# Layer 0's ConvFFN computed in the two phases of layer 1's, on one Trainium2 core

## The chip, the cores and the metric

The kernel runs on one core of a Trainium2 chip. The time is device microseconds of one execution. Two runs of the kernel before gave 3339.99 and 3344.08 us, a median of 3342.03 us. A second kernel is compared by the ratio of its time to that.

## The reference, cut to what matters

Two layers act on 1024 latent tokens and 256 context tokens of width 1024, all in float32. Each layer is an attention followed by a gated ConvFFN, and a norm ends the program. Context tokens go through layer 0 only; after layer 1's attention only the latent tokens are used.

```python
def conv_ffn(t, w_up, w_conv, b_conv, w_down):     # D = 1024, D_FF = 2816
    u = t @ w_up                                   # (n, 2 * D_FF)
    ...
    for tap in range(CONV_W):                      # 3 taps over positions
        acc = acc + up[:, tap:tap + n] * w_conv[tap]
    a, g = jnp.split(acc, 2, axis=-1)
    return (jax.nn.silu(g) * a) @ w_down
...
x = x + g2 * conv_ffn(h2, ...)
if need_ctx:                                       # layer 0 alone
    xc = xc + cg2 * conv_ffn(hc2, ...)
```

## The kernel before, in words

A float32 product is made of three matmuls: each operand is a high and a low part, and high times high, high times low and low times high add up in PSUM. Weights come as tiles of 128 x 1024 from HBM into a `raw` buffer (512 KB, one DMA on SP's queue, L111). Its high part is made by POOL (L123) or by ACT (L121), its low part by a subtraction on POOL (L125); both stand in a split buffer `wsp`. `Weights` keeps a list of what comes next, up to four splits ahead of the one in use; there are three raw and five split buffers. Tokens stand in three blocks of columns: block 0 and block 1 (512 latent tokens each) and block 2 (256 context tokens).

**Layer 0's ConvFFN** (`ffn`, L488) has 22 units of 128 hidden columns. A unit takes an `a` tile and a `g` tile of the up weights, each times all three blocks: `gemm` (L379) issues per tile 8 chunks x 3 matmuls x 3 blocks (512, 512 and 256 columns) into `u`. The three taps and the gate follow on ACT and DVE (`conv` L502 to L507, `gate` L515 to L517). Between the matmuls of the `g` tile stand those of the down product of the unit before (`down_step`, L532): groups of three into `y_ps`, each added to the resident `X` by one DVE instruction (L534). Over all units this is 2112 matmuls of 512 columns and 1056 of 256 for `u`, and 1056 and 528 for `y_ps`. Each down tile passes once. Beside it stand two pieces of work for layer 1. The modulation weights (`ada`) of four sixths are multiplied on DVE (`ada_dve`, L301 and L304), one tile a unit. And `W.sums` loads the `a` and `g` tiles of a layer 1 unit, forms four sums and differences of halves on POOL (L138 to L141) and stores them to `sscr` (L143).

**Layer 1's ConvFFN** works on the 1024 latent tokens alone and in two phases. The up product is formed as seven products of halves instead of eight: halves of the weights' 1024 inputs, and sums of them (`sscr`), meet halves of the tokens and sums of them (`token_forms`: T1 to T4 and B22). For the first 8 units the two products that need no token form (`first`, `second`) run early, into `escr`, while the forms are made; then all units pass in the order `SEQUENCE`, and the gated columns go to `gscr`. The down product (`down`, L1487) runs block by block: eight PSUM banks collect over all 22 units, so the down weights pass once for each block; `end` (L1494) adds the residual, which it loads from `xspill` one chunk at a time.

The order on each engine comes from the scheduler, except on PE (and DVE in layer 1's up phase), where it is the order of the code. SP's queue issues the DMAs in one order, and an issue that waits for a buffer holds what stands behind it.

Of the kernel before, what the change touches and what calls it, by code (L numbers as in the profile page):

```python
# [11 lines left out]
F32 = mybir.dt.float32  # L12
# [35 lines left out]
NE = 8  # L48
SEQUENCE = [x for i in range(NF) for x in (i, NE + i) if x < (NE if x == i else NF)]
NG = 5  # L50
V5 = 4
# [23 lines left out]
BUFS = {"t": 2, "R": 2, "sq": 2}  # L75
# [9 lines left out]
class Weights:  # L85
# [12 lines left out]

    def fill(self):
        while self.todo and len(self.made) < self.ahead and sum(m[1] for m in self.made) < self.whole:  # L100
            for _ in self.load(1):
                pass

    def load(self, pieces):
# [3 lines left out]
        self.count += 1  # L108
        n = src.shape[1]
# [19 lines left out]
    def sums(self, a, g, dst):  # L129

        nc = self.nc
        self.count += 1
        ra, rg = (self.raw_pool.tile([P, 1024], F32, name=f"raw{self.count}{x}", tag="raw") for x in "ag")
        for t, src in ((ra, a), (rg, g)):
            nc.sync.dma_start(out=t, in_=src)
# [21 lines left out]
def _body(nc, tc, es, a, out):  # L157
# [82 lines left out]
    xspill = dram.tile([P, KC, SEQ], F32, name="xspill")  # L240
    sscr = [dram.tile([P, 2048], F32, name=f"sscr{i}") for i in range(NF)]
    escr = [[dram.tile([P, 512], F32, name=f"escr{i}_{k}") for k in range(2)] for i in range(NE)]
    gscr = [dram.tile([P, SEQ], F32, name=f"gscr{i}") for i in range(NF)]
    xscr = dram.tile([P, KC, SEQ], F32, name="xscr")
# [108 lines left out]
    def norm_mod(yp, pool, SS, l, half, b, src, H, R=None, chunks=range(KC), inplace=False):  # L353
# [5 lines left out]
        for kc in chunks:  # L359
            t = src(kc) if inplace else pool.tile([P, 512], F32, name="t", bufs=tb[0])  # L360
            bias = mod[l][:, 24 * half + kc, s:s + 1]
            stt(out=t[:, :n], in0=src(kc), scalar=scale[:, kc, s:s + 1], in1=R[:, :n], op0=ALU.mult, op1=ALU.mult)
            S.activation(out=H[0][:, kc, :], in_=t[:, :n], func=AF.Identity, bias=bias)
            stt(out=H[1][:, kc, :], in0=t[:, :n], scalar=bias, in1=f32(H[0][:, kc, :]), op0=ALU.add, op1=ALU.subtract)  # L364
# [56 lines left out]
    def v_proj(l, bp, vtile, H, half, hook=None, units=None):  # L421
        vu = units or [W.get() for _ in range(4)]
        for i, m in enumerate(tuple(range(KC, NT // P)) + tuple(range(KC)) if ORDER[0][0] == 2 and hook else range(NT // P)):
# [7 lines left out]
    def wo_proj(l, bp, pool, Th, blocks, H, SS, np_, yp):  # L431

        tail = blocks[1:]

        def end(ps, j, b):
            b0, n = BLOCKS[b]
            s = 1 if b0 >= SEQ else 0
            if l == 0:
                xr = pool.tile([P, 512], F32, name="xr", bufs=3)
                nc.sync.dma_start(out=xr[:, :n], in_=a["xT"][:, j, b0:b0 + n])  # L440
            else:
                xr = resid[b][:, j, :]
            stt(out=X[b][:, j, :], in0=ps[:, :n], scalar=mod[l][:, 16 + j, s:s + 1], in1=xr[:, :n],
                op0=ALU.mult, op1=ALU.add)
            if l == 1:
                nc.sync.dma_start(out=xspill[:, j, b0:b0 + n], in_=X[b][:, j, :])
            sumsq(np_, SS, X[b][:, j, :], j, b0, n)

# [1194 lines left out]
```

## Time and profile before

| | us |
|---|---|
| median of two runs (3339.99 and 3344.08) | 3342.03 |
| the profiled execution | 3341.49 |
| its span | 3339.7 |
| PE busy | 3196.2 (96%) |
| DVE, POOL, ACT busy | 2148.2, 1427.6, 1142.3 |

The span runs from the first instruction's start to the last one's end; 1.8 us lie around it. In order of time the stages are: norms, v and qk of layer 0 (to 300 us), its attention (to 848), its output product (to 984.7), its ConvFFN with the first v tiles of layer 1 (to 2031), qk, v and attention of layer 1 (to 2530), its output product (to 2620), its ConvFFN's up phase (to 3064) and down phase (to 3339.7).

### The profile page before, as it was taken

How to read it: one execution, taken by the hardware profiler on the slowest of the kernel's cores; microseconds unless marked ns; L12 is line 12 of the kernel's file. 1: busy time of each engine (PE TensorE's matmuls, PEld its weight loads, DVE VectorE, ACT ScalarE, POOL GpSimd, SP SyncE). 2: the span in 40 equal slices, each digit the busy share in tenths (PEclk: the TensorE clock that was granted, in tenths of full speed). 3: DMA queues.
4: the chain of work that ended last, by engine and by line, in shares of the span. 5: the costliest groups of instructions: out<-in, count | busy, mean ns of one | idle time of the engine just before them, and what ended most of it. 6: DMA issues, size and time to landing. Idle time of an engine off the chain costs nothing.

```text
span 3339.7 us, 43069 instructions
## 1 busy us (share of the span) xinstructions
PE 3196.2 (96%) x15896; PEld 2638.8 (79%) x15896; DVE 2148.2 (64%) x3537; ACT 1142.3 (34%) x1990; POOL 1427.6 (43%) x916
## 2 busy tenths in 40 slices
PE   8999889999989999999999989999999989999988
PEld 4888767777677888888888868888898778888876
DVE  6577388887666666666666684325996667666351
ACT  3121177777222111111111132115994344444011
POOL 2214166666323333333433442222665345446753
PEclk9999999999999999999999999999999999999999
DMA  7564343432422223232322236646884243434452
GB/s 262 166 211 164 126 113 106 115 114 71 142 71 95 101 89 101 90 112 72 115 79 89 89 113 226 237 167 166 194 203 147 98 145 136 149 127 158 164 179 82
DMA packets 213665, 449.47 MB, mean 135 GB/s; under 512 B 25424, under 2 KB 87248, under 8 KB 213456
## 3 DMA queue, kind: packets, MB, share of 16 engines
q1 hardware_dynamic: 212448, 446.41, 41.6%
q8 instruction: 126, 2.06, 0.3%
q14 instruction: 83, 0.68, 0.1%
q10 hardware_dynamic: 1008, 0.32, 0.0%
HBM read 331.28 MB, written 115.34 MB: 134 GB/s over the span
## 4 chain that ended last, share of the span: by engine, by line
PE 62%; DVE 5%; POOL 2%; DMA 2%; issue 1%; ACT 1%; SPq 0%; DVEq 0%; POOLq 0%; ACTq 0%
PE u L379 16%; PE w_ps L1349 11%; PE y_ps L532 9%; PE y_ps L1487 6%; PE qk_ps L379 6%; PE wo_ps L379 4%; PE o L1208 2%; PE wo_ps L464 1%; PE s L1133 1%; PE tl L1160 1%; DVE Hl L364 1%; PE v_ps L391 1%; PE v_ps L390 1%; PE v_ps L389 1%; POOL wsp L125 1%
## 5 line engine op out<-in xcount | busy, mean ns | idle before, releaser
L125 POOL TENSOR_TENSOR wsp<-raw,wsp 128x1024 fp32r<-128x1024 f32 (+2 forms) x283 | 645.3, 2287 | 253.3 <-ACT wsp L121 241.2
L123 POOL TENSOR_SCALAR wsp<-raw 128x1024 fp32r<-128x1024 f32 (+1 forms) x195 | 220.5, 1135 | 1148.0 <-PE u L379 485.5
L379 PE MATMUL u<-Hh,wsp 128*128 128x512 f32 (+1 forms) x2112 | 506.6, 359 | 0.0
L534 DVE SCALAR_TENSOR_TENSOR X<-y_ps,mod,X 128x256 f32<-128x256 f32 (+1 forms) x528 | 343.5, 660 | 247.4 <-PE y_ps L532 246.4
L379 PEld LDWEIGHTS u<-Hh,wsp 128*128 128x128 f32 x2112 | 371.8, 190 | 73.4 <-issue 0.9
L532 PE MATMUL y_ps<-Gh,wsp 128*128 128x512 f32 (+1 forms) x1040 | 365.0, 365 | 12.8 <-DVE X L534 11.9
L379 PE MATMUL qk_ps<-Hh,wsp 128*128 128x512 f32 (+1 forms) x1408 | 329.4, 365 | 0.0
L502 ACT ACTIVATE acc<-u,c_ffn_conv 128x1024 f32<-128x1024 f32 (+2 forms) x89 | 73.7, 875 | 681.2 <-PE u L379 681.0
L379 PE MATMUL u<-Hl,wsp 128*128 128x512 f32 (+1 forms) x1056 | 278.1, 359 | 0.0
L379 PEld LDWEIGHTS qk_ps<-Hh,wsp 128*128 128x128 f32 x1408 | 239.9, 188 | 43.8
L1349 PE MATMUL w_ps<-FT,wsp 128*128 128x512 f32 x1056 | 252.4, 393 | 4.8 <-DVE t L1415 4.8
L532 PEld LDWEIGHTS y_ps<-Gh,wsp 128*128 128x128 f32 x1040 | 198.8, 191 | 56.3 <-DVE X L534 16.3
L1487 PE MATMUL y_ps<-g,wsp 128*128 128x512 f32 x1056 | 242.8, 392 | 0.0
L1349 PEld LDWEIGHTS w_ps<-FT,wsp 128*128 128x128 f32 x1056 | 199.2, 189 | 49.4 <-DVE t L1415 5.2
L1487 PEld LDWEIGHTS y_ps<-g,wsp 128*128 128x128 f32 x1056 | 199.8, 189 | 42.1 <-issue 0.6
L304 DVE SCALAR_TENSOR_TENSOR ada<-raw,c_cvec,ada 128x512 f32<-128x512 f32 x224 | 178.3, 830 | 58.7 <-DMA raw<-in_ada_w_dram 57.6
L379 PEld LDWEIGHTS u<-Hl,wsp 128*128 128x128 f32 x1056 | 179.4, 190 | 25.7
L812 ACT ACTIVATE E<-E,st 128x1280 f32<-128x1280 f32 x128 | 175.3, 1369 | 68.1 <-DVE st L807 67.2
L532 PE MATMUL y_ps<-Gl,wsp 128*128 128x256 f32 (+1 forms) x520 | 188.7, 363 | 2.2 <-DVE Gl L517 2.2
L822 POOL TENSOR_TENSOR E<-E,E 128x1280 f32<-128x1280 f32 x64 | 188.4, 2943 | 5.3
L379 PE MATMUL qk_ps<-Hl,wsp 128*128 128x512 f32 (+1 forms) x704 | 183.6, 364 | 0.0
L807 DVE CUSTOM_DVE_ANT_0 E<-sl,zero,st 128x1024 f32<-128x1024 f32 x128 | 163.7, 1280 | 20.2 <-PE sl L805 19.7
(317 smaller groups left out, 6215.7 us busy)
## 6 DMA issues: line engine op xcount, KB each, us to landing
raw<-in_ada_w_dram SPq DMA_DIRECT2D x96, 512.0 KB
raw<-in_up_dram SPq DMA_DIRECT2D x66, 512.0 KB
raw<-in_down_dram SPq DMA_DIRECT2D x66, 512.0 KB
raw<-sscr SPq DMA_DIRECT2D x44, 512.0 KB
raw<-in_wqk_dram SPq DMA_DIRECT2D x32, 512.0 KB
q<-qscr SPq DMA_DIRECT2D x256, 64.0 KB
q<-qscr SPq DMA_DIRECT2D x64, 256.0 KB
vscr<-vt SPq DMA_DIRECT2D x56, 256.0 KB
```

What stands on the lines that cost most here:

```text
L123: nc.gpsimd.tensor_scalar(out=sp[:, 0, c:c + n], in0=raw[:, c:c + n], scalar1=1.0, scalar2=1.0, op0=ALU.mult, op1=ALU.mult)
L125: nc.gpsimd.tensor_tensor(out=sp[:, 1, c:c + n], in0=raw[:, c:c + n], in1=f32(sp[:, 0, c:c + n]), op=ALU.subtract)
L304: stt(out=accs[v], in0=tv[:, kk, :], scalar=scol[:, kc, v:v + 1], in1=accs[v], op0=ALU.mult, op1=ALU.add)
L379: T.matmul(out=ps, lhsT=w[:, kc, :], rhs=H[b][s][:, kc, :], start=(kc == 0 and i == 0), stop=(kc == KC - 1 and i == 2))
L502: S.activation(out=acc[:, x0:x1], in_=u[:, x0 - t0:x1 - t0], func=AF.Identity, scale=w[:, 1:2], bias=w[:, 3:4])
L532: T.matmul(out=y[:, :n], lhsT=w[:, j, :], rhs=g[:, b0 - g0:b0 - g0 + n], start=(i == 0), stop=(i == len(seq) - 1))
L534: stt(out=x, in0=y[:, :n], scalar=mod[l][:, 40 + j, s:s + 1], in1=x, op0=ALU.mult, op1=ALU.add)
L807: V.tensor_tensor_reduce(out=E[j][:, :SEQ], in0=ps, in1=zero.broadcast_to([P, SEQ]), op0=ALU.add, op1=ALU.min, scale=-1.0, scalar=m, accum ...
L812: S.activation(out=E[j], in_=E[j], func=AF.Exp, scale=-1.0, bias=m, accum_out=sm)
L822: G.tensor_tensor(out=E[0], in0=E[0], in1=E[1], op=ALU.add)
L1349: T.matmul(out=ps, lhsT=w, rhs=form(kc, s), start=(start and kc + i == 0), stop=(kc == 3 and i == 2), skip_group_check=not start)
L1487: T.matmul(out=ys[j], lhsT=w[:, j, :], rhs=g[:, k % 4, s, :], start=(k == 0 and i == 0), stop=(k == NF - 1 and i == 2))
```

## The change

One function `ffn` now serves both layers, with these parts for layer 0.

**Phase A**, 22 units: the pair of tiles is loaded (`add_pair`), high parts on ACT, low parts on POOL (`high_low`, L150 and L151). 48 matmuls of 256 columns make the context's columns. For the first 11 units the early products follow (24 of 512 columns), and the pair's four sums go from the raw tiles to `sscr` (`sums`, L185 to L190).

**Phase B**: the seven-product up of the latent tokens in the order 11, 0, 12, 1, ... A unit below 11 has 60 matmuls of 512 columns; one from 11 on has 84, and its sums are made on POOL as its tiles pass (`add_forms`), with no store.

**Phase C**: the down product by blocks, in the order 2, 0, 1, so that the down weights pass three times. The `ada` tiles are multiplied in blocks 2 and 0 (`ADA_AT`), the sums for 8 units of layer 1 are made in block 1 (`SUM_AT`). Block 1 begins with `turn` (the `ada` columns), a norm and `write0` (layer 1's first operand).

`u` and `y_ps` of layer 0 become `w_ps`: 1848 matmuls of 512 columns and 1056 of 256 for the up product (before 2112 and 1056); the down product keeps 1056 and 528.

In layer 1 the sums of the units from 8 on are now made as their tiles pass. In both layers the residual of block 0 and block 1 is loaded into `X` at the start of the block, and gated tiles use two rotating buffers (six before). The output products load `X` for both blocks at their start. After layer 0's ConvFFN high parts are made on ACT.

```diff
-NE = 8
-NG = 5
-V5 = 4
+NE = (11, 8)
+RAW = 3
+SEQUENCE = [[x for i in range(NF) for x in (ne + i, i) if x < (ne if x == i else NF)] for ne in NE]
+NG = 4
+ADA_AT = [(0, 6), (0, 12)] + [(1, k) for k in range(3, 17)]
+SUM_AT = [(2, k) for k in range(2, 18, 2)]
+V5 = 1
...
+    def halves(self, kind, i, a, g, dst, raw):
+        tt = self.nc.gpsimd.tensor_tensor
+        if i == 0:
+            raw.extend(self.pair(a, g))
+        ra, rg = raw[:2]
...
+        if kind == "pair":
+            self.high_low(raw[i], 1024)
+            if i and dst is not None:
+                self.sums(ra, rg, dst)
+            return
+        if i == 0:
+            raw.append(self.sum_pool.tile([P, 1024], F32, name=f"sum{self.count}", tag="sum"))
+            s = raw[2]
+            tt(out=s[:, 512:], in0=g1, in1=g2, op=ALU.add)
+            tt(out=s[:, :512], in0=s[:, 512:], in1=a1, op=ALU.subtract)
+        elif i == 1:
+            tt(out=a1, in0=a1, in1=g1, op=ALU.subtract)
+            tt(out=a2, in0=a2, in1=raw[2][:, :512], op=ALU.subtract)
+        self.high_low((raw[2], ra, g2)[i] if i < 2 else g2, (1024, 1024, 512)[i])
...
-            x = X[b0 // 512][:, j, :]
-            stt(out=x, in0=y[:, :n], scalar=mod[l][:, 40 + j, s:s + 1], in1=x, op0=ALU.mult, op1=ALU.add)
...
-                gemm(units[1], H, outs[1], extra if ops else None)
...
-                for k in range(i, NF if i == NF - 2 else i + 1):
-                    W.sums(a["up"][1, k], a["up"][1, NF + k], sscr[k])
...
+            for i in range(NF if l == 0 else ne):
+                aa = W.get()
+                if l == 0:
+                    gg, ps = W.get(), bank(1)
+                    for k, u in enumerate((aa, gg)):
+                        gemm(u, H, [(2, ps[:, CTX * k:CTX * k + CTX])])
...
+                if i < ne:
+                    x, p1 = first(aa)
+                    late.append((i, aa, x, p1))
...
+                def end(j):
+                    if b < 2:
+                        x = out_[b][:, j, :]
+                    else:
+                        x = small()[:, :n]
+                        nc.sync.dma_start(out=x, in_=xspill[l][:, j, b0:b0 + n])
+                    stt(out=x, in0=ys[j][:, :n], scalar=mod[l][:, 40 + j, b // 2:b // 2 + 1], in1=x, op0=ALU.mult, op1=ALU.add)
+                    if l == 0:
+                        nc.sync.dma_start(out=xscr[:, j, b0:b0 + n], in_=x)
...
+                for k in range(2, NF - 3):
+                    sp = W.get()
+                    load_g(1)
+                    for j in range(KC):
+                        down(k, j, sp)
+                    if hook:
+                        hook(at, k)
...
+        for i in range(NF if l == 0 else NE[1]):
+            if l == 0:
+                W.add_pair(a["up"][0, i], a["up"][0, NF + i], sscr[0][i] if i < NE[0] else None)
...
+        for i in SEQUENCE[l]:
+            if i < NE[l]:
+                for src in (sscr[l][i][:, :1024], sscr[l][i][:, 1024:], a["up"][l, NF + i][:, 512:]):
+                    W.add(src)
+            else:
+                W.add(a["up"][l, i])
+                W.add_forms(a["up"][l, i], a["up"][l, NF + i])
+        for at in range(3 - l):
+            for k in range(NF):
+                W.add(a["down"][l, k])
+                if l == 0 and (at, k) in ADA_AT:
+                    add_quarters(q1, 1)
```

Three places show how instructions move. On POOL, in the middle of layer 0's ConvFFN, a unit of before has three high parts (L123), three low parts (L125) and the four sums of a layer 1 unit that has tiles of its own:

```order
257 L123 TENSOR_SCALAR wsp_10915<-raw_10913 128x1024
258 L125 TENSOR_TENSOR wsp_10915<-raw_10913,wsp_10915 128x1024
259 L138 TENSOR_TENSOR raw113g<-raw113g 128x512
260 L139 TENSOR_TENSOR raw113g<-raw113a,raw113g 128x512
261 L140 TENSOR_TENSOR raw113a<-raw113g,raw113a 128x512
262 L141 TENSOR_TENSOR raw113a<-raw113a 128x512
```

On POOL in phase A of the change, two units:

```order
253 L151 TENSOR_TENSOR wf_9903<-raw99a,wf_9903 128x1024
254 L151 TENSOR_TENSOR wf_9906<-raw99g,wf_9906 128x1024
255 L185 TENSOR_TENSOR raw99g<-raw99g 128x512
256 L186 TENSOR_TENSOR raw99g<-raw99a,raw99g 128x512
257 L187 TENSOR_TENSOR raw99a<-raw99g,raw99a 128x512
258 L188 TENSOR_TENSOR raw99a<-raw99a 128x512
259 L151 TENSOR_TENSOR wf_10017<-raw101a,wf_10017 128x1024
```

The sums now overwrite the tiles (`raw99a`, `raw99g`) whose low parts PE waits for, and the high parts are gone from POOL. SP's queue for a unit of before issues the pair of a layer 1 unit, its four stores and the unit's own four tiles:

```order
411 L135 DMA raw113a<-in_up_dram 128x1024
412 L135 DMA raw113g<-in_up_dram 128x1024
413 L143 DMA sscr_131<-raw113g 128x512 x2
414 L143 DMA sscr_131<-raw113a 128x512 x2
415 L111 DMA raw_11229<-in_up_dram 128x1024
416 L111 DMA raw_11234<-in_up_dram 128x1024
417 L111 DMA raw_11239<-in_down_dram 128x1024
```

and in phase A of the change (`sscr` are the stores of the sums, `escr` and `gscr` those of the early products and of the context's gated columns):

```order
430 L190 DMA sscr_8_179<-raw97g 128x512 x2
431 L190 DMA sscr_8_179<-raw97a 128x512 x2
432 L156 DMA raw99g<-in_up_dram 128x1024
433 L156 DMA raw101a<-in_up_dram 128x1024
434 L668 DMA escr_7_0_204<-p_9977 128x512
435 L650 DMA gscr_7_134<-t 128x256
436 L668 DMA escr_6_1_203<-t 128x512
437 L190 DMA sscr_9_180<-raw99g 128x512 x2
```

The `g` tile of the next unit is issued behind the four stores of this one. On DVE a unit of before ends with the taps (L507), the gate and the additions to the resident `X`:

```order
1520 L507 SCALAR_TENSOR_TENSOR acc<-u_9969,c_ffn_conv,acc 128x255
1521 L515 TENSOR_TENSOR acc<-acc 128x1280
1522 L517 TENSOR_TENSOR Gl<-acc,Gh 128x1280
1523 L534 SCALAR_TENSOR_TENSOR X_7909<-y_ps,mod_90,X_7909 128x256
1524 L507 SCALAR_TENSOR_TENSOR acc<-u_10287,c_ffn_conv,acc 128x1023
```

and at the passage from block 2 to block 0 of phase C in the change (L776 is the end of one PSUM bank of block 2, L1237 a step of the `ada` product, L555 the low part of a gated tile of block 0, L375 the sum of squares):

```order
1712 L1237 SCALAR_TENSOR_TENSOR rows<-raw_14544,c_cvec,rows 128x512 x2
1713 L776 SCALAR_TENSOR_TENSOR t<-w_ps,mod_90,t 128x256
1714 L1237 SCALAR_TENSOR_TENSOR rows<-raw_14544,c_cvec,rows 128x512
1715 L375 TENSOR_TENSOR SS<-SS,sq 128x256
1716 L1237 SCALAR_TENSOR_TENSOR rows<-raw_14544,c_cvec,rows 128x512
1717 L776 SCALAR_TENSOR_TENSOR t<-w_ps,mod_90,t 128x256
1718 L555 TENSOR_TENSOR g_14395<-t,g_14395 128x512 x4
1719 L375 TENSOR_TENSOR SS<-SS,sq 128x256
1720 L1237 SCALAR_TENSOR_TENSOR rows<-raw_14665,c_cvec,rows 128x512 x2
1721 L776 SCALAR_TENSOR_TENSOR t<-w_ps,mod_90,t 128x256
```

Between the ends of the eight banks stand `ada` steps and gated tiles of the next block.

## Rows read from the trace of the kernel before

**Rows 1.** Windows: length, then busy us and count of each engine, granted clock, DMA:
```profile
core 0: us, PE busy (x) PEld busy (x) DVE busy (x) ACT busy (x) POOL busy (x), PEclk, DMA share, GB/s
984.70:2031.00 1046.30, 1014.33 (x5094) 851.68 (x5093) 684.32 (x925) 176.84 (x214) 388.03 (x245) 0.98 0.28 96
...
2620.00:3064.00 444.00, 428.89 (x1842) 350.19 (x1841) 295.00 (x315) 197.61 (x257) 203.93 (x88) 0.97 0.40 138
3064.00:3339.70 275.70, 251.86 (x1093) 206.44 (x1092) 106.54 (x97) 45.96 (x73) 158.09 (x86) 0.95 0.42 145
```
**Rows 2.** Waits of PE, 984 to 2031 us: total us, times, longest us:
```profile
PE y_ps L532 <- DVE X L534: 14.0, 10, 3.7
PE rn_ps L339 <- DVE SS L327: 7.0, 1, 7.0
```
**Rows 3.** Chain of waits, two stretches of matmuls: start us, us, what and count:
```profile
1890.70 0.69 PE y_ps L532 x3
...
3079.85 91.36 PE y_ps L1487 x403
```
**Rows 4.** Timeline of PE, matmuls of 256 columns: start us, us, what, count:
```profile
985.00 0.28 PE L379 MATMUL u<-Hl,wsp 128*128 128x256 f32 x1
985.12 0.40 PE L379 MATMUL u<-Hh,wsp 128*128 128x256 f32 x2
```
**Rows 5.** Groups by line and shape: count, then busy us, mean ns, idle before:
```profile
L125 POOL TENSOR_TENSOR wsp<-raw,wsp 128x1024 fp32r<-128x1024 f32 x237 | 600.7, 2540 | 228.0 <-ACT wsp L121 217.5
...
L534 DVE SCALAR_TENSOR_TENSOR X<-y_ps,mod,X 128x512 f32<-128x512 f32 x352 | 259.6, 749 | 159.2 <-PE y_ps L532 159.0
...
L304 DVE SCALAR_TENSOR_TENSOR ada<-raw,c_cvec,ada 128x512 f32<-128x512 f32 x224 | 178.3, 830 | 58.7 <-DMA raw<-in_ada_w_dram 57.6
...
L534 DVE SCALAR_TENSOR_TENSOR X<-y_ps,mod,X 128x256 f32<-128x256 f32 x176 | 84.9, 483 | 88.2 <-PE y_ps L532 87.4
...
L121 ACT CAST wsp<-raw 128x1024 fp32r<-128x1024 f32 x66 | 69.3, 1050 | 67.0 <-PE w_ps L1349 60.2 <-issue 6.7
...
L1297 DVE TENSOR_TENSOR g<-t,g 128x512 fp32r<-128x512 f32 x39 | 55.7, 1486 | 8.5 <-ACT g L1296 8.5
```
**Rows 6.** Timeline of POOL, the sums of one unit:
```profile
1588.43 1.30 POOL L138 TENSOR_TENSOR raw153g<-raw153g 128x512 f32<-128x512 f32 x1 [13.16 <-DMA raw153g<-in_up_dram]
1589.81 1.30 POOL L139 TENSOR_TENSOR raw153g<-raw153a,raw153g 128x512 f32<-128x512 f32 x1
...
1592.56 1.30 POOL L141 TENSOR_TENSOR raw153a<-raw153a 128x512 f32<-128x512 f32 x1
```
**Rows 7.** Timeline of SP's DMA issues, the same unit:
```profile
1584.68 0.33 SPq L135 DMA_DIRECT2D raw153g<-in_up_dram  x1
...
1592.50 1.70 SPq L143 DMA_DIRECT2D sscr<-raw153a  x2
1594.30 3.06 SPq L111 DMA_DIRECT2D raw<-in_up_dram  x2
```
**Rows 8.** Windows around PE's wait of 3.7 us, columns as in the first group:
```profile
1039.50:1046.00 6.50, 3.44 (x15) 2.36 (x13) 6.50 (x6) 1.22 (x2) 4.71 (x2) 0.81 0.00 0
1046.00:1060.00 14.00, 14.00 (x61) 11.65 (x62) 9.94 (x15) 0.00 (x0) 5.18 (x4) 0.85 0.53 189
```
**Rows 9.** Waits of PE, 2620 to 3340 us:
```profile
PE rn_ps L339 <- DVE SS L327: 17.7, 3, 10.6
```
**Rows 10.** Chain of waits, the end of the 10.6 us wait:
```profile
3196.92 0.33 SPq L111
...
3197.34 3.90 DMA t<-xspill
```
**Rows 11.** Timeline of DVE, one addition of 128 x 512 at two places:
```profile
969.18 0.68 DVE L327 TENSOR_TENSOR SS<-SS,sq 128x512 f32<-128x512 f32 x1
...
981.76 2.88 DVE L327 TENSOR_TENSOR SS<-SS,sq 128x512 f32<-128x512 f32 x1
```
**Rows 12.** Timeline of POOL beside the second of them:
```profile
981.38 2.71 POOL L125 TENSOR_TENSOR wsp<-raw,wsp 128x1024 fp32r<-128x1024 f32 x1
```

More of the change, by code (lines that the diff above doesn't have):

```diff
@@ L47 @@
 NS = 7
[L48 to L51 removed]
+NE = (11, 8)
+NP1 = (2, 4)
+RAW = 3
[4 more added lines that the diff above has]
+V5 = 1
 NEB = 5
@@ L97, in add, with add_pair, add_forms @@
         self.todo.append((src, split))
+    def add_pair(self, a, g, dst=None):
+        raw = []
+        self.todo.extend((("pair", i, a, g, dst, raw), None) for i in range(2))
+    def add_forms(self, a, g):
+        raw = []
+        self.todo.extend((("forms", i, a, g, None, raw), None) for i in range(3))
     def fill(self):
@@ new lines, in ada_columns, with norm1 @@
+    def ada_columns():
+        for n in range(4):
+            ps = yp.tile([P, 512], F32, name="ada_ps", tag="y")
+            for j in range(4):
+                for v in range(2):
+                    c = 2 * (2 * j + v)
+                    T.matmul(out=ps[:, c:c + 2], lhsT=rows[0][:, 2 * n + v, j * P:j * P + P], rhs=ones[:, :2],
+                             start=True, stop=True)
+            ada_end(1, n, ps[:, :16].rearrange("p (j v c) -> p j v c", v=2, c=2)[:, :, :, 0], 2)
+    def norm1(b, R, x):
+        norm_mod(yp, np_, SS, 1, 0, b, x, H1[b], R, inplace=True)
@@ L1340, in write @@
             nc.sync.dma_start(out=out[:, kc, 512 * b:512 * b + 512], in_=x[:, kc, :])
-    def bank():
-        return bp.tile([P, 512], F32, name="w_ps", tag="b")
-    def product(ps, sp, c, form, start):
-        for kc in range(4):
-            h, l = (sp[:, s, (4 * c + kc) * P:(4 * c + kc + 1) * P] for s in range(2))
-            for i, (w, s) in enumerate(((h, 0), (h, 1), (l, 0))):
-                T.matmul(out=ps, lhsT=w, rhs=form(kc, s), start=(start and kc + i == 0), stop=(kc == 3 and i == 2),
-                         skip_group_check=not start)
@@ L1455, in _body @@
-    while rest:
-        fill()
-    manual.close()
-    gtags = ("T2", "T1", "Hh0", "Hl0", "Hh1", "Hl1")
-    loads = deque((b, k) for b in range(2) for k in range(NF))
-    gs, Rs, xo = {}, [], []
-    def load_g(n, eng=V):
-        for _ in range(n):
-            if not loads:
-                return
-            b, k = loads.popleft()
-            if k % 4 == 0:
-                gs[b, k // 4] = hp.tile([P, 4, 2, 512], F32R, name=f"g{k // 4}", tag=gtags[k // 4])
-            t = small()
-            nc.sync.dma_start(out=t, in_=gscr[k][:, 512 * b:512 * b + 512])
-            split(gs[b, k // 4], k % 4, t, eng)
```

746 lines of the change are left out of this document (341 added, 405 removed).

## Prediction

> **What bounds the kernel now.** I read the windows by stage first [rows 1]. In the stretch of layer 0's ConvFFN (984.7 to 2031 us, with the first v tiles of layer 1) PE is busy for 1014.3 of 1046.3 us, while DVE has 684 and POOL 388. So PE sets the time there, and matmuls taken away count in full unless something else comes late. What a matmul costs is its distance from the next one, not its busy time (busy spans overlap). In the chain of waits, 403 matmuls of 512 columns take 91.36 us, 0.2267 each, and in the ConvFFN of layer 0 three take 0.69, 0.23 each [rows 3]. Matmuls of 256 columns follow each other after 0.12 us, with a new weight tile each [rows 4].
>
> By these the stretch needs 3408 x 0.2267 (2112 u, 1056 y, 240 v) + 1584 x 0.12 + some 10 us of small ones = 973 us. It takes 1046.3, so 73 us are lost: 21 in the two longest kinds of wait [rows 2], some of it to the clock behind them [rows 8], the rest to slightly wider distances and the end of the stage. The question is whether the new form loses more or less than 73.
>
> **What is removed.** The up product keeps 1848 of 2112 wide matmuls: 264 x 0.2267 = 59.9 us (60.7 at 0.23). All else on PE stays: 1056 + 528 narrow ones, 1056 wide ones down, the ada columns. The stretch needs 913 us. On DVE the 352 + 176 additions to X go (260 + 85 us [rows 5]); they were mostly beside PE's work, so I cost them at nothing beyond the 14.0 us of waits that PE had for them, which are in the 73. The 22 high parts per pass go to ACT at 1.05 us, which has 177 of 1046 us filled: nothing.
>
> **What is added, and where it may be late.** I go through the phases and price the losses that replace the 73.
>
> *Phase A, units 0 to 10.* PE needs 48 x 0.12 + 24 x 0.2267 = 11.2 us a unit. One unit's tiles go through a chain, since the sums overwrite both tiles and the next g tile is issued behind the four stores: 0.44 from the last sum's end (1593.86) to the next issue, 3.75 from issue to POOL's first use (1584.68 to 1588.43), 1.05 on ACT, 2.54 of subtraction, and 5.43 for four sums (1588.43 to 1593.86) [rows 5 to 7]. That is 13.2 us, and up to a microsecond more because two loads start together. Nine units at 2 to 3 us over PE are 18 to 27 us; the two units that are ready at the start cover some 10. I take 13 (0 to 32: no wait if the chain overlaps better, and 32 in the rival below).
>
> *Phase A, units 11 to 21.* PE needs 5.76 us, POOL 2 x 2.54 = 5.1, three raw buffers (3.75 + 1.05 + 2.54) x 2 / 3 = 4.9. Nothing is left over: 5 us (0 to 19).
>
> *Phase B.* Two steps need 144 x 0.2267 = 32.6 us on PE; POOL has at most seven subtractions and four sums, 17.8 + 5.5 = 23.3 us. Covered. For the last token forms before it and the start I put 3 + 5 us (2 to 18).
>
> *Phase C, block 2.* A unit is 24 x 0.12 = 2.88 us, POOL 2.54, the buffers 7.34 / 3 = 2.45. The down weights now come three times, and this is where the pace is highest: 6 us (0 to 20; the far end is a rival).
>
> *From block 2 to block 0.* PE's next banks wait for the ends of block 2. On DVE these stand between ada steps (the order shows two to four before each), a group of four gated tiles, and sums of squares; each ada tile is issued on SP behind the store of an earlier end. From the last unit's first bank on, DVE has about 14 steps x 0.83 + 4 x 1.49 + 8 x 0.48 + 8 x 0.4 = 25 us, and at least two load times of 3.75 in series on top [rows 5 to 7]: the eighth bank comes at about 33 us. PE could use it at 8.6 + 7 x 1.36 = 18 us. Loss 14 us (0 to 25).
>
> *Block 0 behind it.* A unit is 5.44 us; DVE has 4 x 0.83 + 1.49 = 4.8, and that wait has given the loads a lead: 4 (0 to 30). *Block 1*: eight pairs for layer 1, each 13.2 us a pair against 10.9 for two units, less a lead of about 16: 5 (0 to 24). *turn, norm and the first operand*: 6. *End of the stage and start*: 6 + 4, as before.
>
> The sum is 13 + 5 + 8 + 6 + 14 + 4 + 5 + 6 + 10 = 71 us, about the 73 of before. So nearly the whole 60 us stays: 60 + 2 = 62.
>
> *Layer 1.* PE waits 10.6 us for the sum of squares in its down phase [rows 9], and the chain behind that wait ends in a residual load (issue at 3196.92, then 3.90 us of transfer) that SP issued late [rows 10]. Now the residual is there from the start of the block, and what remains (an end, a square, an addition, some 2 us) lies under the four banks that PE does first: minus 10. The sums that units 8 to 21 now make on the way add 5.5 us of POOL to steps of 84 x 0.2267 = 19 us, of which POOL holds 8.7: covered. So minus 10 (minus 14 to plus 5). The output products: 0 (minus 2 to plus 3).
>
> Against the profiled execution: 3341.5 - 62 - 10 = 3269.5 us. The median of the runs is 0.5 above it, so **3270 us**.
>
> **Where the skill and the trace meet.** After PE's wait of 3.7 us at 1039.5 us the granted clock is 0.81 and then 0.85 over 14 us [rows 8], that is, part of the time at 1.2 GHz instead of 2.4. [...] The same addition on DVE takes 0.68 us at one place and 2.88 at another, where POOL's subtraction runs from 981.38 for 2.71 us [rows 11, 12]. The Trainium skill, "SBUF — State Buffer", section "Who interferes with whom", says that a DVE instruction with two SBUF inputs and a GpSimd one that reads SBUF exclude each other for a whole instruction; the trace agrees. Both speak against this change and are rivals below.
>
> **The rivals.**
> 1. *All is hidden.* The chains run under PE as they do in layer 1's up phase, where PE is busy for 428.9 of 444 us [rows 1], and 30 us are lost: 3229 us. Against it: the 13.2 us of chain against 11.2.
> 2. *The raw buffers bound phase A and block 1.* The second of the two loads in rows 7 was issued 2.7 us after the first, when a store of the tile had landed (3.06 us for two issues of 0.33). If each cycle waits for that, it is 15.9 us: phase A 9 x 4.7 - 10 = 32 instead of 13, its second half 7.5 a unit instead of 5.76 (19 instead of 5), block 1 19 more. 52 us are given back: 3322. Against it: the order has the a tile one unit ahead, so one load alone is late.
> 3. *DVE is held by POOL in block 0.* Each unit there has one subtraction of 2.54. If an ada step meets it each time, DVE needs 4.8 + 2.5 = 7.3 us against 5.44: 14 x 1.9 = 26 instead of 4, so 3292.
> 4. *The clock.* If waits keep the granted clock at 0.85 through the second half of phase A, block 2 and block 0 (63 + 63 + 120 us), these take 1/0.85 of their time, 43 us more: 3313. Against it: where a chain is the bound, slower matmuls only fill the wait.
> 5. *Slower than before: the down weights come one at a time.* SP's queue in phase C holds gated tiles, stores and ada tiles between them. If they keep only one weight load under way in block 2, a unit takes 3.75 + 1.05 + 2.54 = 7.34 us instead of 2.88: 22 x 4.46 = 98 us more, 3368. It decides from 6.2 us a unit (72 / 22 above 2.88). Against it: three buffers, and loads that the order has ahead.
>
> That the change doesn't remove the matmuls can be left out: the code has 264 fewer.
>
> **How the numbers follow.** The forecast has 0.55, with a range of its own of 3245 to 3298 (the terms of 13 and 14 us at their ends). Rival 1 has 0.12, rival 2 0.15, rival 3 0.08, rival 4 0.06, rival 5 0.04. The range is 3222 (rival 1, with a little less lost) to 3330 (rival 2 and 4 within it); below and above lie 0.2. A 2% difference, about what a measurement of this kernel can tell from no change, lies at 3275.2 and 3408.9. The forecast is faster by that in some 0.6 of its cases (0.33), rival 1 always, rival 3 seldom: 0.46. Slower by 2% needs rival 5 and more: 0.02. The rest is 0.52.
>
> **What would show it.** Layer 0's stretch should take about 984 us, 62 less, with u and y_ps replaced by w_ps. Phase A's units should be 13 to 14 us apart from the third or fourth on, with PE waiting for POOL's low part of g. A wait of PE for DVE's L776 should stand between blocks 2 and 0, 10 to 20 us in all. In layer 1's down phase the 10.6 us wait should be gone. The forecast is wrong if units of block 2 take over 4 us, if phase A's first half takes over 170 us (123 without a wait), or if layer 1 loses time to POOL. Were phase B to show waits for POOL, the sums made on the way would be mis-priced.

## The result and the profile after

The changed kernel took 3466.39 us (two runs, 3463.97 and 3468.82) against 3342.03: 1.0372 times the time before, 95% interval 1.0328 to 1.0417. The forecast was 3270, so not even the sign was right. The profiled execution took 3468.82 us, its span is 3467.0, 127.3 us longer than before. By the first matmul of each stage:

| stage | before | after | forecast |
|---|---|---|---|
| layer 0's output product | 138.2 | 157.1 | 138 |
| layer 0's ConvFFN and layer 1's first v tiles | 1046.1 | 1112.8 | 984 |
| layer 1's up phase | 448.0 | 497.0 | 448 |
| layer 1's down phase | 272.0 | 267.6 | 262 |

Between these stages nothing moved by more than 3.2 us. The windows of after split the ConvFFN into its phases; columns as in [rows 1]. In order: the output product of layer 0, phase A's first 11 units, its last 11, phase B, phase C's blocks 2, 0 and 1, then layer 1's up and down:

```profile
843.40:1000.70 157.30, 141.80 (x654) 110.33 (x654) 90.68 (x130) 39.99 (x72) 43.48 (x24) 0.89 0.46 153
...
1000.70:1157.50 156.80, 133.47 (x804) 118.72 (x803) 92.62 (x102) 62.26 (x97) 113.39 (x63) 0.95 0.60 193
1157.50:1220.70 63.20, 63.20 (x529) 63.20 (x528) 35.54 (x47) 34.94 (x50) 52.00 (x24) 1.00 0.63 193
...
1220.70:1660.60 439.90, 390.43 (x1586) 312.17 (x1586) 286.54 (x274) 167.02 (x215) 252.81 (x121) 0.93 0.34 113
1660.60:1744.60 84.00, 68.93 (x529) 67.21 (x528) 42.64 (x43) 32.54 (x48) 57.03 (x25) 0.91 0.73 240
1744.60:1880.90 136.30, 128.10 (x529) 102.52 (x529) 88.94 (x98) 40.59 (x56) 56.64 (x23) 0.94 0.61 203
1880.90:2053.60 172.70, 146.49 (x603) 116.42 (x604) 58.56 (x61) 44.90 (x61) 96.13 (x54) 0.89 0.62 214
...
2702.30:3199.30 497.00, 445.86 (x1860) 361.11 (x1859) 332.92 (x314) 197.51 (x257) 310.08 (x148) 0.95 0.36 117
3199.30:3467.00 267.70, 248.44 (x1078) 203.05 (x1076) 107.95 (x96) 43.44 (x71) 152.53 (x82) 0.96 0.44 148
```

By the prediction's distances PE needs 123, 63, 359, 63, 120 and 120 us in the phases from A to C. Phase B is thus 81 us over its need and block 1 is 53 (some 10 of it the small matmuls that the prediction counted apart). PE is idle for 49.5 us of phase B, and the clock is 0.93 there; layer 1's up phase went from 0.97 [rows 1] to 0.95 and is 49 us longer.

The largest waits of PE in phase A (two rows), phase B (two), block 1 (one) and layer 1's up phase (two): total us, times, longest.

```profile
PE w_ps L608 <- ACT p L620: 11.6, 2, 8.2
PE w_ps L428 <- POOL wf L151: 5.7, 4, 1.9
...
PE w_ps L608 <- DVE work L708: 31.5, 9, 4.3
PE w_ps L608 <- DVE t L696: 18.0, 11, 4.3
...
PE w_ps L767 <- POOL wsp L142: 16.7, 8, 3.3
...
PE w_ps L608 <- DVE work L708: 27.2, 8, 4.3
PE w_ps L608 <- DVE t L696: 11.1, 8, 2.0
```

Phase B's waits are not for POOL, whose work was added, but for DVE: for two additions that read a PSUM bank (L696, L708) in which PE is to go on. The timelines of after show one such wait (POOL, DVE, then PE; start us, length us):

```profile
1411.90 3.39 POOL L151 TENSOR_TENSOR wf<-sum,wf 128x1024 fp32r<-128x1024 f32 x1
1415.25 2.82 POOL L151 TENSOR_TENSOR wf<-raw161a,wf 128x1024 fp32r<-128x1024 f32 x1
...
1413.54 5.08 DVE L630 SCALAR_TENSOR_TENSOR work<-uh,c_ffn_conv,work 128x512 f32<-128x512 f32 x2
1418.73 1.23 DVE L730 TENSOR_TENSOR work<-work 128x1024 f32<-128x1024 f32 x1
1419.87 0.69 DVE L708 TENSOR_TENSOR work<-w_ps,t 128x512 f32<-128x512 f32 x1
...
1430.17 1.53 DVE L630 SCALAR_TENSOR_TENSOR work<-uh,c_ffn_conv,work 128x512 f32<-128x512 f32 x2
...
1414.38 2.88 PE L608 MATMUL w_ps<-FB,wsp 128*128 128x512 f32 x12
1420.70 2.97 PE L608 MATMUL w_ps<-FT,wsp 128*128 128x512 f32 x12 [3.44 <-DVE work L708]
```

Two taps that take 1.53 us with POOL idle (1430.17) take 5.08 beside two low parts on POOL, and the low part of a sum takes 3.39 where [rows 5] has 2.54. Taps, gate and low part have both inputs in SBUF. L708 has one in PSUM and takes its usual 0.69, but stands behind them in DVE's order. PE has one product, 12 x 0.2267 = 2.72 us (here 1414.38 to 1417.2), before it needs the bank back. It comes 3.44 us late.

### The profile page after: what moved, and what is told of

Read it like the earlier page. It is cut to its first block, busy times and chain, and to the rows that moved or that the text cites. A ratio compares the mean times of both kernels' runs of the same rounds, so it can differ in the third digit from the quotient of the medians.

```text
span 3467.0 us, 43539 instructions
## 1 busy us (share of the span) xinstructions
PE 3192.5 (92%) x15632; PEld 2624.0 (76%) x15632; DVE 2130.6 (61%) x3294; ACT 1400.1 (40%) x2388; POOL 1730.6 (50%) x984
## 4 chain that ended last, share of the span: by engine, by line
PE 49%; POOL 16%; issue 13%; DVE 11%; DMA 8%; ACT 3%; SPq 0%; POOLq 0%; ACTq 0%; DVEq 0%
PE qk_ps L428 9%; PE w_ps L767 9%; POOL wsp L142 6%; PE w_ps L608 6%; POOL wf L151 4%; PE wo_ps L428 3%; PE o L1038 3%; PE sl L987 3%; PE o L1429 2%; PE v_ps L438 2%; PE v_ps L439 2%; PE v_ps L440 2%; PE tp L1014 2%; PE w_ps L428 1%; DMA raw<-in_down_dram 1%
## 5 line engine op out<-in xcount | busy, mean ns | idle before, releaser
L767 PE MATMUL w_ps<-g,wsp 128*128 128x512 f32 (+1 forms) x2640 | 575.8, 380 | 50.1 <-POOL wsp L142 23.2
L767 PEld LDWEIGHTS w_ps<-g,wsp 128*128 128x128 f32 x2640 | 474.4, 195 | 150.1 <-POOL wsp L142 28.8
L138 ACT CAST wsp<-raw 128x1024 fp32r<-128x1024 f32 (+1 forms) x213 | 195.0, 928 | 365.1 <-PE w_ps L608 158.2
L428 PE MATMUL qk_ps<-Hh,wsp 128*128 128x512 f32 x1280 | 319.7, 372 | 0.0
L608 PE MATMUL w_ps<-FT,wf 128*128 128x512 f32 x1200 | 288.1, 392 | 4.4 <-DVE t L696 4.3
L608 PEld LDWEIGHTS w_ps<-FT,wf 128*128 128x128 f32 x1200 | 226.5, 189 | 53.9 <-DVE t L696 4.8
L555 DVE TENSOR_TENSOR g<-t,g 128x512 fp32r<-128x512 f32 (+1 forms) x102 | 135.8, 1372 | 211.6 <-ACT g L554 211.6
L630 DVE SCALAR_TENSOR_TENSOR work<-work,c_ffn_conv 128x1023 f32<-128x1023 f32 x88 | 170.9, 1943 | 98.1 <-ACT work L627 97.2
L608 PE MATMUL w_ps<-Hh,wsp 128*128 128x512 f32 x528 | 177.6, 402 | 8.4 <-ACT p L620 8.4
L987 PE MATMUL sl<-kst,q 128*128 128x512 f32 x512 | 160.0, 436 | 1.6 <-DVE st L989 1.5
```

Source lines behind the costliest of these rows:

```text
L138: nc.scalar.copy(out=sp[:, 0, c:c + n], in_=raw[:, c:c + n])
L428: T.matmul(out=ps, lhsT=w[:, kc, :], rhs=H[b][s][:, kc, :], start=(kc == 0 and i == 0), stop=(kc == KC - 1 and i == 2))
L555: eng.tensor_tensor(out=form[:, kc, 1, :], in0=x, in1=f32(form[:, kc, 0, :]), op=ALU.subtract)
L608: T.matmul(out=ps, lhsT=w, rhs=form(kc, s), start=(start and kc + i == 0), stop=(kc == 3 and i == 2), skip_group_check=not start)
L630: stt(out=acc, in0=u, scalar=convw[:, l, c, k:k + 1], in1=acc, op0=ALU.mult, op1=ALU.add)
L767: T.matmul(out=ys[j][:, :n], lhsT=w[:, j, :], rhs=g[:, k % 4, s, :], start=(k == 0 and i == 0), stop=(k == NF - 1 and i == 2))
```

## The experiments

Stage times of all runs in us, as in the table above. C2, C0 and C1 are the blocks of phase C, wo the output product of layer 0, and "time" is that of the profiled execution. Each of these kernels was run once, after twice and g1 four times:

| run | wo | A | B | C2 | C0 | C1 | up 1 | time |
|---|---|---|---|---|---|---|---|---|
| after | 157.1 | 220.0 | 440.0 | 84.0 | 136.3 | 172.7 | 497.0 | 3468.8 |
| e1_no_form_sums | 157.0 | 223.1 | 363.2 | 84.3 | 133.9 | 172.5 | 436.0 | 3328.9 |
| e2_reads_first | 157.2 | 223.2 | 380.5 | 81.7 | 133.6 | 171.4 | 449.2 | 3353.9 |
| e3_halves | 151.6 | 227.4 | 410.5 | 83.5 | 136.2 | 168.9 | 480.3 | 3417.0 |
| f1_block1_no_pool | 141.4 | 223.7 | 381.4 | 82.2 | 135.9 | 167.8 | 451.0 | 3345.3 |
| f2_order_and_halves | 138.5 | 227.3 | 363.8 | 82.4 | 136.1 | 170.9 | 443.2 | 3322.9 |
| f3_sums_in_qk | 140.3 | 223.3 | 380.5 | 81.8 | 133.7 | 140.1 | 450.7 | 3330.6 |
| f4_three_p1 | 143.3 | 222.6 | 380.4 | 81.8 | 133.9 | 173.0 | 447.6 | 3341.4 |
| g1_sums_split | 137.4 | 225.9 | 364.5 | 79.8 | 135.4 | 154.8 | 442.5 | 3300.8 |
| g2_phaseA_no_pool_sums | 142.2 | 188.4 | 363.8 | 80.8 | 136.1 | 171.5 | 443.3 | 3287.0 |
| g3_sums_all_qk | 138.1 | 225.4 | 363.7 | 79.9 | 133.6 | 138.7 | 442.9 | 3302.5 |

The kernel before took 3338.31 beside the first group (e), 3342.83 beside the second (f), and 3344.45 (median of seven) beside the third (g).

**e1: the sums on the way left out.**

```diff
-            tt(out=s[:, 512:], in0=g1, in1=g2, op=ALU.add)
...
-        self.high_low((raw[2], ra, g2)[i] if i < 2 else g2, (1024, 1024, 512)[i])
+        self.high_low((rg, ra, g2)[i], (1024, 1024, 512)[i])
```

> The changed kernel, but the four sums that POOL forms as tiles pass (L173 to L177, units from 11 on in layer 0 and from 8 on in layer 1) are left out: the raw tiles stand in for them. In the changed kernel layer 0's phase B took 439.9 us and layer 1's up phase 497. Theory 1 (DVE's taps with two SBUF inputs and POOL's operations exclude each other, so DVE reads a PSUM bank late and PE waits): POOL has 5.5 us less in each such step, phase B 385 to 400 us, layer 1's up phase 455 to 465, whole 3370 to 3390. Theory 2 (the order of DVE's own instructions alone, with the drain before L708, makes the waits): both phases unchanged within 5 us. Theory 3 (weights come late through POOL and the raw buffers): the waits of PE would name POOL and fall; 10 us in each phase at most, since PE's waits there name DVE.

Phase B came down by 76.8 us and layer 1's up by 61, both by more than theory 1 had expected. The window of phase B has PE without a gap, for as many matmuls, and the group of the two taps that stand ahead of L708 is back at its length:

```profile
1223.00:1586.20 363.20, 363.20 (x1588) 296.63 (x1587) 258.42 (x272) 166.55 (x213) 183.22 (x80) 1.00 0.42 137
```
```profile
L622 DVE SCALAR_TENSOR_TENSOR work<-uh,c_ffn_conv,work 128x512 f32<-128x512 f32 x88 | 65.6, 746 | 1.5
```

The same group in after, and in before:

```profile
L630 DVE SCALAR_TENSOR_TENSOR work<-uh,c_ffn_conv,work 128x512 f32<-128x512 f32 x88 | 125.5, 1426 | 1.5
```
```profile
L1368 DVE SCALAR_TENSOR_TENSOR work<-uh,c_ffn_conv,work 128x512 f32<-128x512 f32 x44 | 35.8, 813 | 0.7
```

The 76.7 us between the two windows of phase B are 49.5 of idle PE and 27.2 of longer busy time (390.43 against 363.20), at 0.93 and 1.00 of the clock. The sums cost all that the two stages lost.

**e2: the additions that PE waits for before the taps.** This keeps every sum and changes only the order on DVE.

```diff
                 product(y, f, 0, of("T2"), True)
-                fill()
                 V.tensor_tensor(out=u2, in0=y, in1=p1, op=add)
+                fill(3)
...
                 product(y, f, 0, of("T3"), False)
-                while rest:
-                    fill()
                 V.tensor_tensor(out=ug[:, hi], in0=y, in1=q, op=add)
+                fill(0)
```

> The changed kernel with another order on DVE in the seven-product phase: the additions that read PSUM (L696, L700, L708) come before the leftover taps of the step before, instead of behind them. Same work on every engine. Theory 1: DVE's taps stay as long as they are (mean 1.4 us for 512 columns of uh), but they no longer stand before the reads; phase B 400 to 425 instead of 439.9, layer 1's up phase 465 to 485 instead of 497. Theory 2: all waits of that kind go, phase B 365 to 380, layer 1's up phase 440 to 450, and taps are as long as in the kernel before. Theory 3: no change.

Phase B fell by 59.5 us and layer 1's up by 47.8. Neither theory had it whole: the times are about those of theory 2, but the taps do not get shorter as it had them, they are longer than in after:

```profile
L630 DVE SCALAR_TENSOR_TENSOR work<-uh,c_ffn_conv,work 128x512 f32<-128x512 f32 x88 | 152.5, 1733 | 1.6
```
```profile
PE w_ps L608 <- DVE t L693: 4.3, 1, 4.3
PE w_ps L608 <- ACT p L620: 4.0, 8, 0.5
PE w_ps L608 <- DVE work L703: 2.8, 8, 0.5
```

So the length of the taps is not the price. What costs is a lengthened tap that stands ahead of a read of PSUM which PE waits for.

**e3: low parts in halves of 512 columns**, so that POOL holds DVE for less at a time; the order is that of after.

```diff
-        nc.gpsimd.tensor_tensor(out=sp[:, 1, :], in0=src, in1=f32(sp[:, 0, :]), op=ALU.subtract)
+        for c in range(0, n, 512):
+            nc.gpsimd.tensor_tensor(out=sp[:, 1, c:c + 512], in0=src[:, c:c + 512], in1=f32(sp[:, 0, c:c + 512]), op=ALU.subtract)
```

> The changed kernel with each low part on POOL made in two halves of 512 columns (all low parts after layer 0's attention): POOL's total rises by some 0.2 us a tile, its longest single instruction falls from 2.5 to 1.3 us. Theory 1: a DVE instruction waits for at most half as long a POOL instruction, so PE's waits on DVE in phase B (49.5 us) fall by a third to a half: phase B 415 to 425, layer 1's up phase 475 to 485. Theory 2: no change. Theory 3 (POOL's throughput): phase B and block 1 a little slower, 2 to 10 us.

It took 29.5 us off phase B, somewhat more than expected, and 16.7 off layer 1's up: less than half of what the order gives.

**e4: the kernel before, with its layer 1 sums made on the way** (units 8 to 21), nothing else of the change. **g4: the kernel before, with e2's order.**

```diff
             W.add(a["up"][1, i])
+            W.add_forms(a["up"][1, i], a["up"][1, NF + i])
+            continue
```

> The kernel before with one part of the change alone: in layer 1 the sums of units 8 to 21 are made on POOL as their tiles pass; layer 0 makes only the first 8 units' sums. Layer 1's up phase took 447.8 us before and 497 in the changed kernel. Theory 1: 483 to 500 us, and DVE's taps from SBUF grow as in the changed kernel; layer 0's ConvFFN (1046 us) unchanged or up to 5 us shorter; whole 3375 to 3395. Theory 2: unchanged, 3335 to 3345. Theory 3: 455 to 465, with waits of PE for POOL.

> The kernel before, with only the order on DVE changed in layer 1's up phase (reads of PSUM before leftover taps). There POOL makes no sums, and PE's waits for DVE are 4.8 us in all. If the order matters only together with POOL's sums, the up phase stays at 440 to 449 us (448.0 before) and the whole within 0.3% of before; if the order is worth something by itself, 425 to 438.

e4 took 3387.7 us, 49.4 more than the kernel before beside it. Layer 1's up went from 448.0 to 502.3 us, while layer 0's ConvFFN, rid of 14 units' sums, gained only 9.0 (1037.1). The up phase is just over the range of theory 1. The same two waits are there as in after:

```profile
PE w_ps L1395 <- DVE work L1473: 24.9, 7, 4.3
PE w_ps L1395 <- DVE t L1461: 17.2, 8, 7.8
```

g4 took 3339.43 us, layer 1's up 444.8. That is 3.2 us less than before, no more than the 3.4 by which four runs with the same up phase differ (e2, f1, f3 and f4: 447.6 to 451.0). The order decides where POOL makes sums beside the taps; without them no gain of it is shown.

**f1 to f4** all have e2's order, and the first tiles of the output product's weights issued ahead of its other loads (`W.fill()` before `Th`). In after these stood on SP behind the loads of the attention's result; the timeline of SP's issues, of after and then of before:

```profile
842.29 13.29 SPq L1214 DMA_DIRECT2D ots<-oscr  x14
855.67 0.39 SPq L489 DMA_DIRECT2D X<-in_xT_dram  x1
...
868.81 0.39 SPq L128 DMA_DIRECT2D raw<-in_wo_dram  x1
```
```profile
845.53 0.37 SPq L111 DMA_DIRECT2D raw<-in_wo_dram  x1
```

In all runs with that line (f and g) the output product takes 137.4 to 143.3 us instead of 157.

**f1: block 1 without POOL's sums**, loads and stores kept.

```diff
-            W.sums(*W.pair(a["up"][1, i], a["up"][1, NF + i]), sscr[1][i])
+            ra, rg = W.pair(a["up"][1, i], a["up"][1, NF + i])
+            for k, t in enumerate((ra[:, :512], rg[:, 512:], rg[:, :512], ra[:, 512:])):
+                nc.sync.dma_start(out=sscr[1][i][:, 512 * k:512 * k + 512], in_=t)
```

> Reads first on DVE as in the run of that name (whole 3352 us span, output product of layer 0 157.2 us, block 1 of phase C 171.4 us of which PE's matmuls need some 128), and two more edits in other stages. (1) The first four weight tiles of layer 0's output product are issued ahead of the loads of the attention's outputs. If SP's queue order made that stage longer (138.2 before, 157.2 in the changed kernel), it takes 138 to 146; if the four 1 MB loads of X or ACT are at fault, 152 to 158. (2) In block 1 the eight pairs are loaded and stored, but the four sums on POOL are left out. If POOL's time bounds block 1 (two low parts and four sums, some 10.6 us of 10.9 for two units), it takes 130 to 140; if the three raw buffers and the wait for the stores bound it, 155 to 172. Whole: 3290 to 3315 by POOL and queue, 3335 to 3350 by the rivals.

Block 1 took 167.8 us, against 171.4 in e2. POOL's sums are not its bound. The issues of f1 on SP show its pace:

```profile
1904.13 0.33 SPq L128 DMA_DIRECT2D raw<-in_down_dram  x1
1905.04 0.38 SPq L156 DMA_DIRECT2D raw278a<-in_up_dram  x1
...
1911.24 0.33 SPq L128 DMA_DIRECT2D raw<-in_down_dram  x1
...
1919.23 0.33 SPq L128 DMA_DIRECT2D raw<-in_down_dram  x1
1920.13 0.38 SPq L156 DMA_DIRECT2D raw280a<-in_up_dram  x1
```

Two down tiles are issued every 15.1 us (1904.13 to 1919.23), where PE needs 10.9 for two units. A pair holds two of the three raw buffers until its four stores are through. POOL's timeline of f1 has the low parts of the down tiles:

```profile
1901.74 2.37 POOL L142 TENSOR_TENSOR wsp<-raw,wsp 128x1024 fp32r<-128x1024 f32 x1 [5.92 <-ACT wsp L138]
1908.81 2.40 POOL L142 TENSOR_TENSOR wsp<-raw,wsp 128x1024 fp32r<-128x1024 f32 x1 [4.70 <-ACT wsp L138]
1916.85 2.35 POOL L142 TENSOR_TENSOR wsp<-raw,wsp 128x1024 fp32r<-128x1024 f32 x1 [5.64 <-ACT wsp L138]
```

Each of the three issues of a down tile above comes 0.02 or 0.03 us after the end of such a low part (1904.11, 1911.21 and 1919.20), that of the tile before. So the down tiles pass one at a time: load, high part and low part of one take 7.1 to 8.0 us here, and two of them make the 15.1. That the pair's two buffers are what keeps the next load back fits this, and f3 below has no pairs there, but no run had a fourth buffer.

**f3: the eight units' sums moved to layer 1's qk product.**

```diff
-SUM_AT = [(2, k) for k in range(2, 18, 2)]
+SUM_AT = []
...
+            W.sums(*W.pair(a["up"][1, g], a["up"][1, NF + g]), sscr[1][g])
```

> Reads first on DVE, the output product's weights issued first, and the eight pairs of layer 1's sums moved from block 1 of phase C to the qk stage of layer 1, one for each of its eight steps (POOL is lightly used there). Block 1 135 to 142 instead of 171.4. The qk stage takes 261 us up to the attention; if its raw buffers and DMA have room for 16 MB more it stays within 3 us, if not it grows by 10 to 30 (three raw buffers, 21.6 us of holding times in 25.7). Whole 3295 to 3320.

Block 1 fell to 140.1 us, 31 less, but the stretch from the qk product to the attention went from 261.3 to 282.5: two thirds of the gain are paid back.

**f4: a third buffer for the saved early product** (`NP1 = (3, 4)`), against the 8.2 us wait of PE for the copy L620 in phase A.

> Reads first on DVE, the output product's weights issued first, and three instead of two buffers for the saved first products in layer 0. In phase A (223.2 us, 186.6 needed) PE waits 13.2 us for the copy of a first product (L620), 9.0 at once. If that copy waits for the store of an older one, phase A takes 212 to 216; if it waits for something else (ACT's or SP's order), 220 to 224. Whole 3325 to 3340.

Phase A took 222.6 us, as before: a miss. The copy does not lack a buffer. It stands in ACT's order behind casts that themselves waited for their tiles (timelines of ACT and then PE in after):

```profile
1146.22 1.04 ACT L150 CAST wf<-raw103g 128x1024 fp32r<-128x1024 f32 x1 [5.03 <-DMA raw103g<-in_up_dram]
...
1149.38 1.04 ACT L150 CAST wf<-raw105a 128x1024 fp32r<-128x1024 f32 x1 [1.63 <-DMA raw105a<-in_up_dram]
...
1152.43 0.58 ACT L620 COPY p<-w_ps 128x512 f32<-128x512 f32 x1
...
1153.06 0.80 PE L608 MATMUL w_ps<-Hh,wf 128*128 128x512 f32 x1 [8.21 <-ACT p L620]
```

**f2: the order, the weights first, and halves.**

> Reads first on DVE, the output product's weights issued first, and all low parts on POOL in halves. With the order repaired, what a DVE tap waits for POOL no longer stands before a PSUM read, so halves should give little: phase B 375 to 383 (380.5 without), layer 1's up phase 445 to 452 (449.2). If the length of POOL's instructions still matters to PE, phase B 365 to 372. Whole 3325 to 3345.

With the order mended, halves still gave 16.7 us in phase B and some 6 in layer 1's up (449.2 to 443.2), more than I had thought. Phase B is at 363.8 us, which is what e1 has without any sums. In phase A they cost some 4 us (223.2 to 227.3).

**g1 to g3** start from f2. g1 leaves four of the eight units' sums in block 1 and makes four in the qk product, g3 makes all eight there. What was expected of g1 and then of g3:

```diff
+SUM_AT = [(2, k) for k in range(2, 18, 4)]
...
+            if g % 2:
+                m = 4 + g // 2
+                W.sums(*W.pair(a["up"][1, m], a["up"][1, NF + m]), sscr[1][m])
```

> The changed kernel with reads first on DVE, low parts in halves, the output product's weights issued first, and layer 1's eight pairs of sums divided: four in block 1 of phase C, four in the qk stage of layer 1. With all eight in block 1 it took 3322.9 us (block 1 170.9, qk and v stage 261.3 up to the attention); with all eight in the qk stage block 1 was 31 us shorter and the qk stage 21 longer. If each place has some room (a lead of some 16 us in block 1, unused buffers in qk), four in each cost less than half: block 1 142 to 152, qk stage 262 to 270, whole 3298 to 3315. If the cost goes by the pair, block 1 155, qk 272, whole 3315 to 3322. Either way faster than the kernel before by 0.6% or more.

> As the run with the sums divided, but all eight pairs in the qk stage. Block 1 138 to 142, qk stage 278 to 284, whole 3308 to 3316.

g1 took 3301.65 us (median of four) against 3344.45, 0.9882 of the time before, interval 0.9860 to 0.9905. Its stretch from the qk product to the attention still takes 261.3 us, better than expected, and block 1 is 16 us shorter than in f2, no better than the cost by the pair; in g3 the 32 us of block 1 cost 20.4 in that stretch (281.7). The one run of g3 (3302.45) lies among the four of g1 (3297.70 to 3311.28), so which of the two is better is not shown by the whole time.

g2 keeps phase A's loads and stores and leaves out POOL's sums there.

```diff
-                self.sums(ra, rg, dst)
+                for k, t in enumerate((a1, g2, g1, a2)):
+                    self.nc.sync.dma_start(out=dst[:, 512 * k:512 * k + 512], in_=t)
```

> The changed kernel with reads first on DVE, low parts in halves and the output product's weights issued first; in phase A the four sums of units 0 to 10 are left out on POOL (the raw tiles are stored in their place, so that loads and stores stay). Phase A took 227.3 us with the sums, PE's matmuls need 186.6. If the chain of a unit (load, high part, low part, sums, store, next load; 13.3 us apart in the trace of the changed kernel) sets the time, it is now some 8 to 9 us a unit, below PE's 11.2: phase A 190 to 202. If the waits for the copy of a first product (ACT's order) or the pace of the loads set it, 215 to 228. The other stages stay.

```profile
989.70:1178.10 188.40, 188.40 (x1330) 177.34 (x1329) 96.89 (x149) 97.62 (x148) 120.75 (x88) 1.00 0.66 211
```

Phase A falls from 227.3 to 188.4 us, its need of 187 and a little less than expected, and PE has no gap. There the chain through POOL's sums is the bound, and not the loads and stores; in block 1 leaving out the sums changed almost nothing.

## Why the prediction was wrong

*Matmuls removed, 60 us.* Right: with the sums and their effects away, the phases come to their need by the distances of [rows 3] and [rows 4] (g2's 188.4 of 186.6, e1's 363.2 of 359.2). The gain was there and was given back.

*Phase B, "covered", 8 us.* This is the step that failed: 81 us were lost. I added up POOL's time alone (23.3 of 32.6 us) and called it cover. But POOL's low parts and sums and DVE's taps exclude each other, as [rows 11, 12] had shown: 0.68 and 2.88 us for one addition. I used that for block 0 only (rival 3), and not where PE waits for DVE within 2.72 us. The sum of the two engines would not have shown the loss either. By the shortest lengths in after's phase B (low parts 2.39 and 1.28, sums 1.25, taps 1.27 and 0.74, gate 1.22) I estimate for two units 19.6 us of POOL and 11.9 of DVE work with both inputs in SBUF: 31.5 of PE's 32.6 us. One after the other that just fits, and in f2 it did (363.8 us). What the step left out is that PE needs single reads on time: e2 changes only their place and gives back 59.5 of the 81 us. The Trainium skill, "SBUF — State Buffer", section "Who interferes with whom", has the rule, and the trace agrees (1.53 and 5.08 us for the same taps). The text itself named what would show the sums mis-priced: waits for POOL in phase B. They came as waits for DVE instead. Its other sign, that layer 1 loses time to POOL, did come.

*Layer 1's up, "covered", 0.* The same step; it measured +49. e4 shows this in the kernel before as well, without layer 0's part. The down phase was to gain 10 us and gained 4.4. The wait of 10.6 us is gone [rows 9]; its longest is 5.0 now. But the rest was not hidden under the four banks as I had it: PE still waits 7.3 us there for the sum of squares.

*Phase A, 13 + 5.* The pace was right and the sum was not. The two `g` tiles in the rows below are issued 13.3 us apart, against a chain of 13.2, and g2 confirms what sets it. But the first 11 units lost 34 us, not 13. PE's waits for the low part of a `g` tile, which I had priced, are 5.7 us in four; its waits for ACT's copies (11.6 us, of which 8.2 behind two ACT casts) and for DVE's taps (5.0) were not in the sum, and the clock was 0.95, so that PE was busy for 133 us with 123 us of work. The second 11 lost nothing (63.2).

```profile
1129.06 0.37 SPq L156 DMA_DIRECT2D raw101g<-in_up_dram  x1
...
1142.38 0.37 SPq L156 DMA_DIRECT2D raw103g<-in_up_dram  x1
```

*Blocks 2 and 0, 6 + 14 + 4 = 24.* They are 37 us over their need; here the size was off by half. The wait for L776 between them, forecast at 10 to 20 us, came to 5.1 us in three, with one of 6.8 for a gated tile on ACT (L554) beside it. What makes up the rest was not tested.

*Block 1, 5 us, and 6 for turn and norm.* Some 43 us were lost beside the small matmuls. f3 takes 31 of them away by moving the loads, sums and stores, and f1 shows that the sums on POOL are not what they wait for. The 15.1 us a pair are near the 15.9 of rival 2, which I had at 19 us more here and gave 0.15. But its mechanism, a second load of the pair issued 2.7 us late, is not there: the two loads are issued 0.47 us apart in f1 and 0.48 in after. In f1 the down tiles pass one at a time, which is rival 5's mechanism, with 7.1 to 8.0 us for its 7.34; I had it in block 2 alone and gave it 0.04. In phase A the pace was 13.3 us, so rival 2 did not hold there either.

*Output product, 0 (minus 2 to plus 3).* It lost 19 us, to the place of its first weight loads on SP's queue. I priced the operations of that stage and did not walk its queue.

*The rivals.* The time lies outside all five. Rival 3 had the right mechanism in the wrong stage. Rival 4 had the clock as an effect of waits, in phases A and C; it came in phase B too, 27 us beside 49.5 of waiting. Rival 5 did not happen in block 2, which took 84 us for 22 units, 3.8 each.

The account: 66.7 us in the ConvFFN (where minus 62 was forecast), 49 in layer 1's up, 19 in the output product, minus 4.4 in the down phase and minus 3.2 ahead of the output product make 127.

## What to carry to other kernels

Where work is moved to POOL beside a DVE that works from SBUF, add the two engines' times as one, to see whether any room is left. Then look which DVE instruction PE waits for, since the sum does not show that: put the reads of PSUM ahead of the long SBUF work, and cut POOL's instructions short. A change that pays in matmuls can be right in its arithmetic and lose by the order of what surrounds it; here four small edits of order and place turned a loss of 3.7% into a gain of 1.2%. For each moved load walk the whole queue that it now stands in, since the cost of its place is not in any price of an operation.

## What the hardware showed that I had not expected

The exclusion lengthens both sides: the two taps 1.53 to 5.08 us, the low part of a sum from 2.54 to 3.39. By itself it need not cost PE anything. In e1, where POOL makes low parts alone, the two taps keep 746 ns, but other taps meet the low parts: those that read a saved product in SBUF take 1738 ns, and 741 where the same tap reads PSUM. PE has no gap in phase B.

```profile
L622 DVE SCALAR_TENSOR_TENSOR work<-t,c_ffn_conv,work 128x511 f32<-128x511 f32 x38 | 66.0, 1738 | 0.0
...
L622 DVE SCALAR_TENSOR_TENSOR work<-w_ps,c_ffn_conv,work 128x511 f32<-128x511 f32 x50 | 37.0, 741 | 0.0
```

Some twenty waits of up to 4.3 us went with a granted clock of 0.93 over a phase of 440 us, between its two levels of 1.2 and 2.4 GHz; without the waits it was 1.00 (e1). The lower clock cost 27 us on top of 49.5 of waiting, more than half as much again.

Dividing a POOL instruction in two was worth 16.7 us in phase B even with the order mended (e2 to f2), though it adds instructions: POOL was busy for 281.81 us there against 253.51, and PE nevertheless had almost no gap:

```profile
1212.00:1575.00 363.00, 361.19 (x1583) 296.58 (x1582) 269.48 (x272) 163.34 (x213) 281.81 (x178) 1.00 0.42 139
```

The largest loss left in g1 is phase A, 225.9 us against g2's 188.4. Making its sums in another place was not tried.
